# Operand address differences for TensorE, and the root of the first feed-forward, in a two-layer decoder trunk

## The chip, the cores and the metric

The kernel runs on 1 core of a Trainium2 chip. The metric is the device time of one execution in microseconds (us), lower is better.

## The reference, cut to what matters

```python
D_MODEL, SEQ, DEPTH, D_FF = 1024, 512, 2, 2816

def rms_norm(x, g):
    y = x * lax.rsqrt(jnp.mean(x * x, axis=-1, keepdims=True) + 1e-6)
    return y * g
def swiglu(x, wg, wu, wd):
    return (jax.nn.silu(x @ wg) * (x @ wu)) @ wd

for i in range(DEPTH):
    x = x + 0.5 * swiglu(rms_norm(x, ffn1_norm[i]), ffn1_w_gate[i], ffn1_w_up[i], ffn1_w_down[i])
    h = rms_norm(x, mix_norm[i])
    x = x + (conformer_conv(h, ...) if i % 2 == 0 else nsa_mixer(h, ...))
    x = x + 0.5 * swiglu(rms_norm(x, ffn2_norm[i]), ffn2_w_gate[i], ffn2_w_up[i], ffn2_w_down[i])
    gate = jax.nn.sigmoid(rms_norm(x, ple_norm[i]) @ ple_w_gate[i])
    x = x + gate * (p[i] @ ple_w_in[i])
return rms_norm(x, final_norm)
```

So there are four feed-forwards (two in each layer), one convolution module with a 31-tap depthwise filter, one block of sparse attention with three branches, two gates on a per-layer input, and a last norm. All of it is float32.

## The kernel before, in words

The activations are kept transposed: eight tiles of 128 features by 512 tokens (`self.xs`). Weights come from HBM in units of 128 x 1024 floats (4096 bytes in each partition) that `plan()` lays out in the order of use.

**Three matmuls for one.** TensorE multiplies in fp32r. Each float is therefore split into a high part (a copy into fp32r, on ScalarE) and a low part (the difference, on VectorE or GpSimd), and `mm3` (L360 to L365) issues three matmuls for each product: high by high (L363), weight high by activation low (L364), weight low by activation high (L365). The weight block (128 x 128) is the stationary operand and is loaded anew for each matmul; the activations (512 or 256 tokens) are the moving operand. The split weights stand in `wh` and `wl`, five buffers each (L299, L301, L323, L324).

**Full-size and half-size.** A plain product moves 512 tokens. In a feed-forward the first two column blocks of gate and up (`PLAIN = 2`) are plain. The other twenty go two by two through `pairs` (L502), seven products of half size in place of eight (Winograd's form of Strassen's scheme): its moving operands have 256 tokens. They are the high and low parts of the inputs (`s`, in slots), and sums of inputs `T1` to `T4` that `right_sums` (L482) makes (`px`). Its stationary operands are weight units ("s"), combinations of two units ("c" and "d", made in `combine` from the sums of `first_sums`), and a sum "e" that stands in a tile of its own, `s1hl`. The down products move 512 tokens of `hid`.

**Where operands stand.** An allocator stacks the pools one behind the other in each partition: constants, weights (2 + 5 + 5 buffers of 4096 bytes), a gap of 64 bytes (`gap0`), 24 slots of 2048 bytes, the small tiles of a norm (`tiny`, 832 bytes), a gap of 192 bytes (`gap1`), and then the pool of the phase, with gaps of 64 bytes ahead of `s1hl` and 192 ahead of `G` and `hid` (`PADS`). Taken modulo 256 bytes, the address of the moving operand less that of the stationary one is 64 for `s` and `px` against `wh` and `wl`, 192 for `px` against `s1hl`, and 0 for `hid` against `wh` and `wl`. Other tiles fall where they fall: the convolution's result (`tw`) against `wh` and `wl` has 32, the per-layer input (`zp`) 160, the attention's `e` tiles any multiple of 32, the probabilities against V 32.

**The order.** The program is written engine-neutral; a scheduler orders each engine's instructions by its own simulation, priorities (`high_priority`) and explicit constraints: `issue_after(x)` keeps what is inside behind instruction x in the order. All engines then work through fixed queues.

**The first feed-forward.** `ffn` (L550) of layer 0 starts on data straight from HBM. `rfin` (L468) has two steps: sums over features of the squares by eight small matmuls (`token_sums`, L452), plus epsilon on VectorE (L474), the power -0.5 on GpSimd (`rsqrt`, L445); then four transposes on TensorE that spread the root over the partitions (L458) and a copy (L465). The sums stand behind the third input of block 1's gate product (`SUMS_AT = 3`), the transposes behind the end of that product. The four `right_sums` come behind the last square and behind L474 (`vins`). `gated` (L565 to L568) multiplies and splits the plain blocks' results. `ahead` (L341) splits the weight units that come next, as far as the five buffers go.

Of the kernel before, what the change touches and what calls it, by code (L numbers as in the profile page):

```python
# [24 lines left out]
PAD_SLOTS, PAD_PHASE = 16, 48  # L25
PADS = {"s1hl": 16, "G": 48, "hid": 48}
# [11 lines left out]
SUMS_AT = 3  # L38
# [159 lines left out]
class Kern:  # L198
    def __init__(self, ctx, tc, aps):
        self.ctx, self.tc, self.nc = ctx, tc, tc.nc  # L200
        self.a = aps
        pool = lambda name, **kw: ctx.enter_context(tc.tile_pool(name=name, **kw))
        self.cpool = pool("consts", bufs=1)
        self.wpool = pool("weights", bufs=1)
        pool("gap0", bufs=1).tile([128, PAD_SLOTS], F32, name="gap0")
        self.spool = pool("slots", bufs=1)
        self.tiny = pool("tiny", bufs=2)
        pool("gap1", bufs=1).tile([128, PAD_PHASE], F32, name="gap1")
# [5 lines left out]
        self.HLB, self.held, self.now = 5, set(), None  # L214
        self.next_raw = self.next_split = 0
# [9 lines left out]

    def ptile(self, tag, n, w=512, dt=F32):
        if tag in PADS and tag not in self.padded:
            self.padded.add(tag)
            self.phase.tile([128, PADS[tag]], F32, name=f"gap{tag}{self.uid}", tag=f"gap{tag}", bufs=1)
        self.uid += 1  # L230
        return self.phase.tile([128, w], dt, name=f"{tag}{self.uid}", tag=tag, bufs=n)
# [38 lines left out]
    def halves(self):  # L270
        h = self.wpool.tile([128, HU], F32R, name=f"wh{self.uid}", tag="wh", bufs=self.HLB)
        l = self.wpool.tile([128, HU], F32R, name=f"wl{self.uid}", tag="wl", bufs=self.HLB)
        self.uid += 1
        return h, l

    def _split(self, what, j):
        nc = self.nc
        w = sum(x[2] for x in UNITS[j])
        if what == "r":
            t = self.wpool.tile([128, HU], F32, name=f"wr{j}", tag="wh", bufs=self.HLB)  # L280
# [10 lines left out]
        h, l = self.halves()  # L291
        name = UNITS[j][0][0][0]
        nsa, calm = name.startswith("nsa"), name.startswith(CALM)
        eng = nc.gpsimd if calm or nsa and j % 4 in L_POOL else nc.vector
        for c in self.pieces(j, w):
            if nsa and j % 4 in H_POOL:
                nc.gpsimd.tensor_copy(h[:, c], t[:, c])
            else:
                nc.scalar.activation(h[:, c], t[:, c], AF.Copy)  # L299
# [11 lines left out]
    def combine(self, what, j):  # L311


        nc = self.nc
        t, u = self.raw[j], self.raw[j + 1]
        lo, hi = slice(0, HU // 2), slice(HU // 2, HU)
        q = self.sums[j]
        if what == "c":
            nc.vector.tensor_tensor(q[:, lo], u[:, lo], t[:, lo], op=OP.subtract)
            nc.vector.tensor_tensor(u[:, lo], t[:, hi], q[:, lo], op=OP.subtract)  # L320
        src = q if what == "c" else u
        h, l = self.halves()
        nc.scalar.activation(h, src, AF.Copy)  # L323
        nc.vector.tensor_tensor(l, src, h.bitcast(F32), op=OP.subtract)  # L324
        self.hl[what, j] = (h, l)

    def first_sums(self, j):

        nc = self.nc
        t, u = self.raw[j], self.raw[j + 1]  # L330
        lo, hi = slice(0, HU // 2), slice(HU // 2, HU)
        q = self.sums[j] = self.ptile("sq", 2, HU)
        with self.tc.issue_after(self.summed):
            nc.vector.tensor_tensor(q[:, hi], t[:, lo], u[:, lo], op=OP.subtract)
        nc.vector.tensor_tensor(u[:, lo], u[:, lo], u[:, hi], op=OP.add)
        hl = self.ptile("s1hl", 2, HU, F32R)
        nc.scalar.activation(hl[:, lo], u[:, lo], AF.Copy)
        nc.vector.tensor_tensor(hl[:, hi], u[:, lo], hl[:, lo].bitcast(F32), op=OP.subtract)
        self.hl["e", j] = (hl[:, lo], hl[:, hi])

    def ahead(self, e):  # L341
# [3 lines left out]
        self.loads()  # L345
        while self.next_split < e:
# [100 lines left out]

    def token_sums(self, p, tiles):
# [19 lines left out]
    def rfin(self, acc):  # L468

        with self.tc.high_priority(FIN_PRI):  # L470
# [4 lines left out]
            r = self.rsqrt(v, 4)  # L475
# [74 lines left out]
    def ffn(self, n, i, nxt):  # L550
# [4 lines left out]
        fin = self.rfin(self.acc)  # L555
# [5 lines left out]
        for pi, fs in enumerate(PARTS):  # L561
# [9 lines left out]
            if pi == 0:  # L571
                assert PLAIN == 2
                first = (n, i) == (1, 0)
                wait = []
                for f in range(PLAIN):
                    pg, pu = self.bank(), self.bank()
                    if f == 0:
                        for ks in (range(KD - 1), (KD - 1,)):
                            plain(pg, g, f, ks)
                            plain(pu, u, f, ks)  # L580
                    for p, nm in ((pg, g), (pu, u)) if f else ():
                        if first and p is pg:
                            plain(p, nm, f, range(SUMS_AT))
                            with self.tc.issue_after(self.lastmm):
                                next(fin)
                            plain(p, nm, f, range(SUMS_AT, KD))
                        else:
                            plain(p, nm, f)
# [16 lines left out]
                for f, pg, pu in wait:  # L605
                    gr = self.tmp()
                    nc.vector.tensor_tensor(pg, pg, R, op=OP.mult)
                    nc.scalar.activation(gr, pg, AF.Silu)
                    gated(f, gr, pu)
            for f in fs[::2]:  # L610
# [3 lines left out]
                G = next(both)  # L614
# [104 lines left out]
    def glu(self, c, pa, pg, ta=None):  # L719
# [4 lines left out]
        with self.tc.high_priority(FIN_PRI):  # L724
            nc.vector.tensor_tensor(pg, pg, self.R, op=OP.mult)
            nc.scalar.activation(pg, pg, AF.Sigmoid, bias=self.col("conv_b_pw1", KD + c))
            if CONV_ON[c] == "pe":
                u = self.ptile("uu", 2, PH * (SP + LAGS - 1)).rearrange("p (q s) -> p q s", q=PH)
# [4 lines left out]
            else:  # L733
                u = self.ptile("u", 3, S + TAPS - 1)
# [103 lines left out]
    def conv(self, nxt):  # L838
# [3 lines left out]
        self.dwc = self.phase.tile([128, KD, TAPS], F32, name="dwc")  # L842
# [159 lines left out]
    def put_k(self, g):  # L1002
        nc, t, KT = self.nc, self.kt, self.KTs[g % 2]
        for br, sl, ot in ((0, slice(0, 64), slice(64, 128)), (1, slice(64, 128), slice(0, 64))):
            nc.scalar.activation(KT[sl, 0, br, 32:], t[sl], AF.Copy)
            nc.vector.tensor_tensor(KT[sl, 1, br, 32:], t[sl], KT[sl, 0, br, 32:].bitcast(F32), op=OP.subtract)
            nc.sync.dma_start(KT[ot, :, br, 32:].bitcast(F32), KT[sl, :, br, 32:].bitcast(F32))
# [6 lines left out]
    def proj_q(self, g, pr):  # L1014
# [6 lines left out]
        Q = self.phase.tile([128, 2, 512], F32R, name=f"q{g}{pr}", tag="q", bufs=4)  # L1021
# [60 lines left out]
    def cmp_in(self, j, first):  # L1082
# [15 lines left out]
        for gp, p in wait:  # L1098
            for s in range(2):
                t = self.ptile("e", EB, 516)  # L1100
# [54 lines left out]
    def scores(self, job):  # L1155
# [16 lines left out]
        for a in range(HPG):  # L1172
            Q = self.Q[g, a // 2][:, a % 2, qt * 128:qt * 128 + 128]
            src, e = {}, self.slot() if a == HPG - 1 else self.ptile("e", EB, 516)
# [109 lines left out]
    def osplit(self, g):  # L1284
        nc = self.nc
        for pr in range(2):
            t = self.OT[g][pr]
            h, l = (self.slot(F32R) if g < 2 else self.ptile("e", EB, 516, F32R)[:, :512] for _ in range(2))
# [26 lines left out]
    def nsa(self, nxt):  # L1315
# [3 lines left out]
        P = self.phase  # L1319
# [3 lines left out]
        self.pos = P.tile([128, 2, 16], F32, name="pos")  # L1323
        nc.gpsimd.dma_start(self.pos, self.a["pos"])
        self.rowmask = P.tile([128, 1], F32, name="rowmask")
        nc.gpsimd.dma_start(self.rowmask, self.a["rowmask"])
        self.gates = P.tile([128, 4, 48], F32, name="gates")
        self.gates0 = P.tile([128, 16], F32, name="gates0")
        self.kc = P.tile([128, G, 32], F32, name="kc")
        self.ec = P.tile([128, 4, HPG, 32], F32, name="ec")  # L1330
        nc.gpsimd.memset(self.ec, 0.0)
        self.vc = P.tile([128, G, 128], F32R, name="vc")
        self.KTs = [P.tile([128, 2, 2, 544], F32R, name=f"kt{i}") for i in range(2)]
        self.Vs = [P.tile([128, 8, 128], F32R, name=f"v{i}") for i in range(2)]
        self.ects = [P.tile([128, 2, 512], F32R, name=f"ect{i}") for i in range(2)]
# [111 lines left out]
    def run(self):  # L1447
        def phase():
            self.padded = set()
# [4 lines left out]
        for i in range(L):  # L1454
            self.tb = 4
# [84 lines left out]
```

## Time and profile before

| | us |
|---|---|
| median of 3 runs | 1990.7 (1990.41 to 1990.72) |
| the profiled execution | 1990.31 |
| its span, first to last instruction | 1988.2 |
| granted clock of TensorE, mean | 0.997 of full speed |

In the profile PE is TensorE's matmuls, PEld its weight loads, DVE VectorE, ACT ScalarE, POOL GpSimd, SP the engine that issues DMAs. A row of a group says: line, engine, operation, output tile <- input tiles, shape, count, then busy us and mean ns of one, and the idle time before them with what ended it. A row of the timeline says: start in us, length in us, and the same names. The recorded length of a matmul includes its way through the array; how fast matmuls follow each other is read from their starts.

### The profile page before, as it was taken

What the parts mean: (1) busy time and instruction counts of PE and PEld (TensorE: products, weight loads), DVE (VectorE), ACT (ScalarE), POOL (GpSimd) and SP (SyncE); (2) the same over time, 40 slices, a digit from 0 to 9 for tenths busy, and PEclk for the clock granted to TensorE, in tenths of its full rate; (3) what the DMA queues carried; (4) which work ended last, traced back from release to release, by engine and by line L of the source; (5) the groups of instructions that cost most, each with busy time, mean ns of one, the idle gap of its engine ahead of it and who ended that gap; (6) DMA issues with size and microseconds to landing.
All of it is one profiled execution on the core that took longest, in us unless ns stands there. A gap on an engine that the chain in (4) does not pass through costs nothing.

```text
span 1988.2 us, 32709 instructions
## 1 busy us (share of the span) xinstructions
PE 1961.4 (99%) x12534; PEld 1760.0 (89%) x12534; DVE 1544.6 (78%) x2703; ACT 1099.8 (55%) x1972; POOL 331.0 (17%) x365
## 2 busy tenths in 40 slices
PE   8999999999999999999999999999999999999998
PEld 7989898888789898988999989888888789998987
DVE  8869777795688796877978868636889797786875
ACT  7636446663565363545644626337888665363543
POOL 0000000352300000022000000557666200000022
PEclk9999999999999999999999999999999999999999
DMA  4332322566425243343232323463332023232241
GB/s 172 107 106 97 128 86 96 192 206 202 138 99 172 88 151 128 99 138 117 85 126 87 129 84 100 156 196 106 89 96 101 23 94 129 96 117 96 96 149 53
DMA packets 79483, 235.16 MB, mean 118 GB/s; under 512 B 8848, under 2 KB 16160, under 8 KB 79328
## 3 DMA queue, kind: packets, MB, share of 16 engines
q1 hardware_dynamic: 78368, 230.69, 35.4%
q8 instruction: 98, 1.61, 0.3%
q0 software_dynamic: 816, 2.33, 0.3%
q14 instruction: 57, 0.47, 0.1%
q10 hardware_dynamic: 144, 0.07, 0.0%
HBM read 214.66 MB, written 16.29 MB: 116 GB/s over the span
## 4 chain that ended last, share of the span: by engine, by line
PE 90%; DVE 6%; ACT 1%; issue 1%; DMA 1%; SPq 0%; POOL 0%; DVEq 0%; ACTq 0%; POOLq 0%
PE b L363 27%; PE b L364 27%; PE b L365 27%; PE b L828 2%; PE b L1187 1%; PE b L1251 1%; DMA raw<-in_w 1%; PE b L1270 1%; PE b L1271 1%; PE b L1126 1%; DVE s L422 1%; DVE t L489 1%; DVE wl L301 1%; DVE px L498 0%; DVE acc L439 0%
## 5 line engine op out<-in xcount | busy, mean ns | idle before, releaser
L363 PE MATMUL b<-s,wh 128*128 128x256 f32 (+1 forms) x1408 | 443.8, 316 | 2.2 <-ACT wh L299 1.4
L364 PE MATMUL b<-s,wh 128*128 128x256 f32 (+1 forms) x1408 | 440.9, 314 | 1.4 <-DVE s L422 1.2
L365 PE MATMUL b<-s,wl 128*128 128x256 f32 (+1 forms) x1408 | 440.2, 314 | 0.1
L299 ACT ACTIVATE wh<-raw 128x1024 fp32r<-128x1024 f32 (+1 forms) x251 | 263.7, 1053 | 241.8 <-PE b L364 158.4
L364 PE MATMUL b<-px,wh 128*128 128x256 f32 (+1 forms) x1112 | 319.8, 288 | 1.7 <-DVE px L498 1.7
L363 PE MATMUL b<-px,wh 128*128 128x256 f32 (+1 forms) x1112 | 319.4, 288 | 0.7 <-ACT G L510 0.7
L365 PE MATMUL b<-px,wl 128*128 128x256 f32 (+1 forms) x1112 | 319.6, 288 | 0.0
L301 DVE TENSOR_TENSOR wl<-raw,wh 128x1024 fp32r<-128x1024 f32 (+1 forms) x205 | 251.6, 1229 | 65.2 <-ACT wh L299 64.8
L363 PEld LDWEIGHTS b<-s,wh 128*128 128x128 f32 x1408 | 264.5, 188 | 21.2 <-ACT wh L299 2.2
L364 PEld LDWEIGHTS b<-s,wh 128*128 128x128 f32 x1408 | 264.3, 188 | 20.4 <-DVE s L422 2.3
L365 PEld LDWEIGHTS b<-s,wl 128*128 128x128 f32 x1408 | 263.4, 188 | 18.6 <-DVE wl L301 0.5
L364 PE MATMUL b<-hid,wh 128*128 128x512 f32 x704 | 273.1, 389 | 0.0
L365 PE MATMUL b<-hid,wl 128*128 128x512 f32 x704 | 272.7, 389 | 0.0
L363 PE MATMUL b<-hid,wh 128*128 128x512 f32 x704 | 269.1, 389 | 0.0
L301 POOL TENSOR_TENSOR wl<-raw,wh 128x1024 fp32r<-128x1024 f32 (+1 forms) x53 | 128.5, 2429 | 695.2 <-ACT wh L299 695.1
L510 ACT ACTIVATE G<-b 128x256 f32<-128x256 f32 x400 | 144.5, 376 | 132.4 <-PE b L365 109.8
L364 PEld LDWEIGHTS b<-px,wh 128*128 128x128 f32 x1112 | 208.7, 188 | 7.1 <-DVE px L498 2.3
L363 PEld LDWEIGHTS b<-px,wh 128*128 128x128 f32 x1112 | 208.4, 188 | 6.1 <-ACT G L510 1.3
L365 PEld LDWEIGHTS b<-px,wl 128*128 128x128 f32 x1112 | 208.8, 188 | 4.0
L364 PEld LDWEIGHTS b<-hid,wh 128*128 128x128 f32 x704 | 132.1, 188 | 27.0
L365 PEld LDWEIGHTS b<-hid,wl 128*128 128x128 f32 x704 | 132.0, 188 | 27.1
L363 PEld LDWEIGHTS b<-hid,wh 128*128 128x128 f32 x704 | 132.1, 188 | 26.9
(246 smaller groups left out, 3621.0 us busy)
## 6 DMA issues: line engine op xcount, KB each, us to landing
raw<-in_w SPq DMA_DIRECT2D x255, 512.0 KB, 3.3
rawx<-in_w SPq DMA_DIRECT2D x80, 512.0 KB, 3.3
tw<-in_tw SPq DMA_DIRECT2D x20, 576.0 KB, 6.6
skew<-table SPq DMA_DIRECT2D x16, 320.0 KB, 5.8
z<-t SPq DMA_DIRECT2D x16, 256.0 KB, 2.4
hid<-z SPq DMA_DIRECT2D x16, 256.0 KB, 3.9
tt<-skew SPq DMA_DIRECT2D x16, 256.0 KB, 2.9
wr<-in_w SPq DMA_DIRECT2D x8, 512.0 KB, 4.0
```

The lines of the kernel that those rows point to most:

```text
L299: nc.scalar.activation(h[:, c], t[:, c], AF.Copy)
L301: eng.tensor_tensor(l[:, c], t[:, c], h[:, c].bitcast(F32), op=OP.subtract)
L363: mm(out, sh, mh, start=start, stop=False, **how)
L364: mm(out, sh, ml, start=False, stop=False, **how)
L365: self.lastmm = mm(out, sl, mh, start=False, stop=stop, **how).ins
L422: b = nc.vector.scalar_tensor_tensor(view(l), x, g, view(h.bitcast(F32)), op0=OP.mult, op1=OP.subtract)
L489: sub = lambda o, x, y: nc.vector.tensor_tensor(o, x, y, op=OP.subtract)
L510: copy = lambda o, x: nc.scalar.activation(o, x, AF.Copy)
L828: nc.tensor.matmul(p[:, q * SP:q * SP + SP], T[q][:, d * 128:d * 128 + 128], u[:, q, o:o + SP], start=d == 0, stop=d == LAGS - 1)
L1126: nc.tensor.matmul(P[mh][:, :124], w, B[kk // 4][:, kk % 4, :], start=kk == 0, stop=kk == 15)
L1187: nc.tensor.matmul(p[:, :32 - lo + nk], Q, KT[:, i, "sw".index(b), lo:32 + nk], start=i == 0, stop=i == 1)
L1251: nc.tensor.transpose(p[:, a * 128:a * 128 + 128], J[a, b][:, kt * 128:kt * 128 + 128], self.ident)
```

## The change

It has two parts.

*Addresses.* Every tile's place is now chosen. `tiny` moves ahead of the weights, a gap of 64 bytes follows it, and slots stand right behind the weights. The split units get 256 bytes more, and a unit made for `pairs` (a "s" unit of a pair, "c" and "d") begins 64 bytes (`TURN` = 16 floats) further on. `place` puts the first tile of a tag at a chosen address modulo 256 (`AT`), and several widths become multiples of 256 bytes (`UW` = 576 floats; KT and the e tiles). With this the moving operand less the stationary one is 192 modulo 256 for all of `pairs`, and 0 for the products of 512 tokens, the convolution's, the per-layer input's and the attention's among them.

*First feed-forward of layer 0.* The root is Newton's iteration on VectorE (ten instructions on 128 x 4) in place of GpSimd's power. The sums of squares move ahead of the eighth input of block 0's two products. The first `right_sums` waits for the sum of squares alone, the other three for the root. Splitting of the first pair's units is held back (`cap`), the sums of its weights (`first_sums`, `sum_parts`) come later (`lazy`), and the gates of the plain blocks come behind the right sums. In layer 0's first phase there are five `t` buffers, not four.

```diff
-PAD_SLOTS, PAD_PHASE = 16, 48
-PADS = {"s1hl": 16, "G": 48, "hid": 48}
+PAD, TURN = 16, 16
+AT = {"s1hl": 192, "px": 128, "hid": 128, "tw": 128, "e": 128, "tt": 0, "q": 0}
+UW = 576
-SUMS_AT = 3
+NEWTON = 3
...
+    def place(self, tag, size, at=None):
+        pad = 0 if at is None else (at - self.top) % 256
+        if pad:
+            self.uid += 1
+            self.phase.tile([128, pad // 4], F32, name=f"gap{tag}{self.uid}", tag=f"gap{tag}", bufs=1)
+        self.top += pad + -(-size // 32) * 32
...
-    def halves(self):
-        h = self.wpool.tile([128, HU], F32R, name=f"wh{self.uid}", tag="wh", bufs=self.HLB)
+    def halves(self, half=False):
+        o = TURN if half else 0
+        h = self.wpool.tile([128, HU + 64], F32R, name=f"wh{self.uid}", tag="wh", bufs=self.HLB)[:, o:o + HU]
...
         if pair:
-            with self.behind():
-                self.first_sums(j)
+            if j not in self.lazy:
+                with self.behind():
+                    self.first_sums(j)
+                    self.sum_parts(j)
...
+        if lazy:
+            with self.tc.issue_after(self.righted):
+                self.sum_parts(j)
+                nc.vector.tensor_tensor(u[:, lo], t[:, hi], q[:, lo], op=OP.subtract)
...
+    def root_steps(self, v, n):
+        y = self.tiny.tile([128, 4], F32, name="r", tag="r")[:, :n]
+        a = self.tiny.tile([128, 4], F32, name="ra", tag="ra")[:, :n]
+        nc.vector.tensor_scalar(y.bitcast(I32), v.bitcast(I32), -0.5, float(0x5f3759df), op0=OP.mult, op1=OP.add)
+        for _ in range(NEWTON):
+            nc.vector.tensor_tensor(a, y, y, op=OP.mult)
+            nc.vector.scalar_tensor_tensor(a, a, -0.5, v, op0=OP.mult, op1=OP.mult)
+            self.root = nc.vector.scalar_tensor_tensor(y, a, 1.5, y, op0=OP.add, op1=OP.mult).ins
...
                         for ks in (range(KD - 1), (KD - 1,)):
                             plain(pg, g, f, ks)
                             plain(pu, u, f, ks)
+                            if first and len(ks) > 1:
+                                with self.tc.issue_after(self.lastmm):
+                                    next(fin)
...
-                        if first and p is pg:
-                            plain(p, nm, f, range(SUMS_AT))
-                            with self.tc.issue_after(self.lastmm):
-                                next(fin)
-                            plain(p, nm, f, range(SUMS_AT, KD))
...
                 if first:
-                    with self.tc.issue_after(self.squared), self.tc.issue_after(self.vins):
-                        for k in range(KD // 2):
+                    for k in range(KD // 2):
+                        with self.tc.issue_after(self.squared), self.tc.issue_after(self.root if k else self.summed):
                             self.right_sums(f"ffn{n}_norm", i, k)
+                        if k == KD // 2 - 2:
+                            self.cap = ENTRY["s", self.lazy[1]] + 1
+                            with self.tc.issue_after(self.root):
+                                self.ahead(ENTRY["s", self.lazy[1]])
+                    self.cap = None
...
+                with self.tc.issue_after(self.root) if first and f == PLAIN else nullcontext():
+                    G = next(both)
+                if first and f == PLAIN:
+                    with self.tc.issue_after(self.righted):
+                        plain_gates()
...
-            self.tb = 4
+            self.tb = 5 if i == 0 else 4
```

More of the change, by code (lines that the diff above doesn't have):

```diff
@@ L213, in __init__ @@
         self.unskewed = []
-        self.HLB, self.held, self.now = 5, set(), None
+        self.HLB, self.held, self.now, self.cap = 5, set(), None, None
+        self.lazy = ()
         self.next_raw = self.next_split = 0
@@ L224, in tmp, with own @@
         return self.ptile("t", self.tb, dt=dt)
+    def place(self, tag, size, at=None):
[4 more added lines that the diff above has]
+        self.top += pad + -(-size // 32) * 32
+    def own(self, name, shape, dt=F32, at=None):
+        size = 4
+        for n in shape[1:]:
+            size *= n
+        self.place(name, size, at)
+        return self.phase.tile(shape, dt, name=name)
     def ptile(self, tag, n, w=512, dt=F32):
-        if tag in PADS and tag not in self.padded:
-            self.padded.add(tag)
-            self.phase.tile([128, PADS[tag]], F32, name=f"gap{tag}{self.uid}", tag=f"gap{tag}", bufs=1)
+        if tag not in self.tags:
+            self.tags.add(tag)
+            self.place(tag, n * (-(-w * 4 // 32) * 32), AT.get(tag))
         self.uid += 1
@@ L290, in _split @@
             del self.raw[j]
-        h, l = self.halves()
+        h, l = self.halves(pair)
         name = UNITS[j][0][0][0]
@@ L316, in combine @@
         lo, hi = slice(0, HU // 2), slice(HU // 2, HU)
+        lazy = what == "c" and j in self.lazy
+        if lazy:
+            self.first_sums(j)
         q = self.sums[j]
@@ L319, in combine @@
             nc.vector.tensor_tensor(q[:, lo], u[:, lo], t[:, lo], op=OP.subtract)
[L320 removed]
+            if not lazy:
+                nc.vector.tensor_tensor(u[:, lo], t[:, hi], q[:, lo], op=OP.subtract)
         src = q if what == "c" else u
[L322 removed]
+        h, l = self.halves(True)
         nc.scalar.activation(h, src, AF.Copy)
@@ L335, in first_sums, with sum_parts @@
         nc.vector.tensor_tensor(u[:, lo], u[:, lo], u[:, hi], op=OP.add)
+    def sum_parts(self, j):
+        nc = self.nc
+        u = self.raw[j + 1]
+        lo, hi = slice(0, HU // 2), slice(HU // 2, HU)
         hl = self.ptile("s1hl", 2, HU, F32R)
@@ L345, in ahead @@
         self.loads()
+        if self.cap is not None:
+            e = min(e, self.cap)
         while self.next_split < e:
@@ L466, in spread, with rfin @@
         return R
-    def rfin(self, acc):
+    def rfin(self, acc, steps=False):
         with self.tc.high_priority(FIN_PRI):
@@ L474, in rfin @@
             self.vins = self.nc.vector.tensor_scalar(v, p, 1e-6, None, op0=OP.add).ins
-            r = self.rsqrt(v, 4)
+            r = (self.root_steps if steps else self.rsqrt)(v, 4)
         yield
@@ L554, in ffn @@
         self.now, self.T4 = (f"ffn{n}", i), []
-        fin = self.rfin(self.acc)
+        first = (n, i) == (1, 0)
+        if first:
+            self.lazy = [PLACE[nm, i, 0, PLAIN][0] for nm in (g, u)]
+            self.cap = ENTRY["s", self.lazy[0]]
+        fin = self.rfin(self.acc, steps=first)
         def plain(p, nm, f, ks=range(KD)):
@@ L604, in ffn, with plain_gates @@
                 R = self.R
[L605 to L609, printed above, removed]
+                def plain_gates():
+                    for f, pg, pu in wait:
+                        gr = self.tmp()
+                        nc.vector.tensor_tensor(pg, pg, R, op=OP.mult)
+                        nc.scalar.activation(gr, pg, AF.Silu)
+                        gated(f, gr, pu)
+                if not first:
+                    plain_gates()
             for f in fs[::2]:
@@ L613, in ffn @@
                 both = self.pairs((g, u), i, f)
-                G = next(both)
+                with self.tc.issue_after(self.root) if first and f == PLAIN else nullcontext():
+                    G = next(both)
+                if first and f == PLAIN:
+                    with self.tc.issue_after(self.righted):
+                        plain_gates()
                 nc.vector.tensor_tensor(G, G, R[:, None, :].to_broadcast([128, 2, 512]), op=OP.mult)
@@ L841, in conv @@
         X, U, Y = self.X, {}, []
-        self.dwc = self.phase.tile([128, KD, TAPS], F32, name="dwc")
+        self.dwc = self.own("dwc", [128, KD, TAPS])
         nc.gpsimd.dma_start(self.dwc, self.a["dwc"])
@@ L1287, in osplit @@
             t = self.OT[g][pr]
-            h, l = (self.slot(F32R) if g < 2 else self.ptile("e", EB, 516, F32R)[:, :512] for _ in range(2))
+            h, l = (self.slot(F32R) if g < 2 else self.ptile("e", EB, UW, F32R)[:, :512] for _ in range(2))
             nc.scalar.activation(h, t, AF.Copy)
@@ L1322, in nsa @@
             nc.gpsimd.dma_start(self.xd[m * 128:m * 128 + 128, :], self.xs[m])
-        self.pos = P.tile([128, 2, 16], F32, name="pos")
+        self.pos = self.own("pos", [128, 2, 16])
         nc.gpsimd.dma_start(self.pos, self.a["pos"])
-        self.rowmask = P.tile([128, 1], F32, name="rowmask")
+        self.rowmask = self.own("rowmask", [128, 1])
         nc.gpsimd.dma_start(self.rowmask, self.a["rowmask"])
[L1327 to L1330, printed above, removed]
+        self.gates = self.own("gates", [128, 4, 48])
+        self.gates0 = self.own("gates0", [128, 16])
+        self.kc = self.own("kc", [128, G, 32])
+        self.ec = self.own("ec", [128, 4, HPG, 32])
         nc.gpsimd.memset(self.ec, 0.0)
[L1332 to L1335, printed above, removed]
+        self.vc = self.own("vc", [128, G, 128], F32R, at=0)
+        self.KTs = [self.own(f"kt{i}", [128, 2, 2, UW], F32R, at=128) for i in range(2)]
+        self.Vs = [self.own(f"v{i}", [128, 8, 128], F32R, at=0) for i in range(2)]
+        self.ects = [self.own(f"ect{i}", [128, 2, 512], F32R, at=0) for i in range(2)]
         for t in self.KTs:
```

36 lines of the change are left out of this document (18 added, 18 removed).

## The prediction

> **What bounds the kernel now.** I read the page first, then the groups of TensorE's instructions by form, the timeline of single matmuls, and last the waits and the timeline of the first 90 us. The page:
>
> ```profile
> span 1988.2 us, 32709 instructions
> PE 1961.4 (99%) x12534; PEld 1760.0 (89%) x12534; DVE 1544.6 (78%) x2703; ACT 1099.8 (55%) x1972; POOL 331.0 (17%) x365
> PE 90%; DVE 6%; ACT 1%; issue 1%; DMA 1%; SPq 0%; POOL 0%; DVEq 0%; ACTq 0%; POOLq 0%
> ```
>
> TensorE has a record at nearly all times, and 90% of the chain that ended last is its own. So the time is the number of matmuls by the distance from one start to the next, plus a few pauses. The change leaves the number alone. The groups by form give the numbers of each kind:
>
> ```profile
> L364 PE MATMUL b<-px,wh 128*128 128x256 f32 x1008 | 278.9, 277 | 1.7 <-DVE px L498 1.7
> L364 PE MATMUL b<-hid,wh 128*128 128x512 f32 x704 | 273.1, 389 | 0.0
> L363 PE MATMUL b<-s,wh 128*128 128x256 f32 x960 | 265.7, 278 | 1.0 <-ACT wh L299 1.0
> L364 PE MATMUL b<-s,wh 128*128 128x512 f32 x448 | 175.9, 393 | 1.4 <-DVE s L422 1.2 <-DVE s L1290 0.2
> L364 PE MATMUL b<-px,s1hl 128*128 128x256 f32 x320 | 88.1, 277 | 0.2 <-DVE px L498 0.2
> L364 PE MATMUL b<-px,wh 128*128 128x512 f32 x104 | 40.9, 393 | 0.0
> L364 PE MATMUL b<-tw,wh 128*128 128x512 f32 x64 | 25.1, 395 | 0.0
> L364 PE MATMUL b<-zp,wh 128*128 128x512 f32 x32 | 12.7, 396 | 0.0
> L365 PE MATMUL b<-e,wl 128*128 128x512 f32 x32 | 12.6, 394 | 0.0
> ```
>
> L363, L364 and L365 have the same counts, so each stands for three. Half-size (256 tokens): 3 x (1008 + 960 + 320) = 6864. Full-size at difference 0 (`hid`): 2112. At 64 (`s`, `px`): 3 x (448 + 104) = 1656. At 32 (`tw`): 192. At other differences (`zp`, `e`): 192.
>
> **The full-size matmuls.** Three undisturbed runs, first and last start of each; there are 133, 167 and 150 steps between the two:
>
> ```profile
> 225.02 0.39 PE L365 MATMUL b<-hid,wl 128*128 128x512 f32 x1
> ...
> 255.16 0.39 PE L363 MATMUL b<-hid,wh 128*128 128x512 f32 x1
> ```
> ```profile
> 908.00 0.39 PE L364 MATMUL b<-px,wh 128*128 128x512 f32 x1
> ...
> 946.23 0.39 PE L365 MATMUL b<-s,wl 128*128 128x512 f32 x1
> ```
> ```profile
> 515.03 0.39 PE L363 MATMUL b<-tw,wh 128*128 128x512 f32 x1
> ...
> 550.03 0.39 PE L363 MATMUL b<-tw,wh 128*128 128x512 f32 x1
> ```
>
> At difference 0: 30.14 us / 133 = 226.6 ns. At 64: 38.23 / 167 = 228.9. At 32: 35.00 / 150 = 233.3. The change takes all to 0. That is worth 1656 x 2.3 = 3.8 us, 192 x 6.7 = 1.3 us, and for `zp` and `e` between 192 x 2.3 and 192 x 6.7, say 0.9: together 6.0 us. A third of the 1656 and the `e` stand in attention, where TensorE also waits for other engines; I take half of their share away and count **5 us**, bounds 3.8 and 6.
>
> The Trainium skill, page "SBUF — State Buffer", section "Who interferes with whom", gives TensorE two independent read ports, one for the moving operand and one for weights, and says that only the port pair of VectorE and GpSimd causes contention. By that rule both address terms are nil. The trace disagrees: 226.6 against 228.9 and 233.3 ns for one shape of matmul.
>
> **The half-size matmuls** have two distances from start to start, and keep either for long. Three stretches of 59, 6 and 23 steps:
>
> ```profile
> 142.08 0.28 PE L364 MATMUL b<-s,wh 128*128 128x256 f32 x1
> ...
> 149.03 0.28 PE L363 MATMUL b<-px,wh 128*128 128x256 f32 x1
> ```
> ```profile
> 149.74 0.28 PE L363 MATMUL b<-px,s1hl 128*128 128x256 f32 x1
> ...
> 150.42 0.28 PE L363 MATMUL b<-px,s1hl 128*128 128x256 f32 x1
> ```
> ```profile
> 1642.69 0.28 PE L363 MATMUL b<-px,s1hl 128*128 128x256 f32 x1
> ...
> 1645.39 0.28 PE L365 MATMUL b<-px,s1hl 128*128 128x256 f32 x1
> ```
>
> The first, at difference 64, is wide: 6.95 us / 59 = 117.8 ns. The second is the `s1hl` product behind it, difference 192: 0.68 us / 6 = 113.3. The later products of that stage stay at 113.3, back at difference 64. By starts, 1643 of the 6864 are wide; the first and the last of them are these:
>
> ```profile
> 35.75 0.28 PE L363 MATMUL b<-s,wh 128*128 128x256 f32 x1
> ...
> 1975.69 0.28 PE L365 MATMUL b<-px,wl 128*128 128x256 f32 x1
> ```
>
> Each stage of pairs begins wide when it comes from full-size products, and the quick pace comes nearly always where `s1hl` begins; no undisturbed stretch falls back. But the third fence is a product at 192 that stays wide: 2.70 us / 23 = 117.4. So 192 does not by itself end a stretch of 117.8 ns; what the trace doesn't show is a stage that *enters* at 192. Bounds: all quick, 1643 x 4.45 ns = 7.3 us won; all wide, (6864 - 1643) x 4.45 = 23.2 us lost. I take the quick end, since 192 is where the pace changed for the better and never for the worse, less 0.5 for matmuls that stand in pauses anyway: **6.8 us** won.
>
> **The first feed-forward.** Its pauses:
>
> ```profile
> PE b L458 <- POOL r L445: 3.8, 2, 2.6
> PE b L364 <- DVE px L498: 1.9, 3, 0.8
> ```
> ```profile
> 23.13:51.50 28.37, 23.70 (x152) 20.56 (x150) 28.30 (x45) 19.31 (x30) 1.41 (x1) 1.00 0.28 94
> 51.50:90.00 38.50, 38.50 (x338) 38.41 (x339) 38.18 (x58) 26.08 (x43) 0.00 (x0) 1.00 0.34 112
> ```
>
> The columns of the second fence are length, then PE, PEld, DVE, ACT and POOL. From 23.13 to 51.5 TensorE has no record for 28.37 - 23.70 = 4.67 us, and VectorE rests for 0.07. VectorE is the limit there, and it still has 38.18 of 38.50 behind. So a gain must come out of its queue:
>
> ```profile
> 19.33 0.62 PE L363 MATMUL b<-s,wh 128*128 128x512 f32 x2
> 19.64 2.28 DVE L439 TENSOR_TENSOR acc<-acc,t 128x512 f32<-128x512 f32 x3
> 23.13 0.69 DVE L334 TENSOR_TENSOR sq<-raw,rawx 128x512 f32<-128x512 f32 x1 [1.21 <-DMA raw<-in_w]
> ```
> ```profile
> 26.19 0.95 PE L452 MATMUL b<-meanr,acc 128*128 128x1 f32 x8
> 28.06 0.16 DVE L474 TENSOR_SCALAR v<-b 128x4 f32<-128x4 f32 x1
> 28.31 1.41 POOL L445 TENSOR_TENSOR r<-v,power 128x4 f32<-128x4 f32 x1 [26.31 <-DVE v L474]
> 29.77 0.65 PE L458 MATMUL b<-ident,r 128*128 128x128 f32 x4 [2.63 <-POOL r L445]
> 35.62 1.29 DVE L607 TENSOR_TENSOR b<-b,R 128x512 f32<-128x512 f32 x2
> 45.24 0.70 DVE L565 TENSOR_TENSOR b<-b,t 128x512 f32<-128x512 f32 x1
> ```
>
> - *Newton.* Ten VectorE instructions by 0.16 us (L474's row, the same size) are 1.6 us, against 1.41 on GpSimd and hops of under 0.1 each way. The root itself takes as long as before; but 1.6 us more stand in the full queue, ahead of everything that waits there.
> - *Sums earlier.* The squares' total is there at 19.64 + 2.28 = 21.92; the sums run at 26.19 and TensorE then waits 2.63 for the root. Before the eighth input is enough to take that wait away. Bound on the other side: the 42 matmuls of block 0's first seven inputs are issued by 19.33, and if the sums stand in TensorE's queue right there, it waits 21.92 - 19.3 = 2.6 for the total, and nothing is won.
> - *Right sums earlier, gates and weight sums later.* The 1.21 us that VectorE waits for a unit's DMA at 23.13 can go to the first right sums. The plain gates (1.29 for both, then L565 and L568, of one size, at 0.70 for each of two blocks: 4.1 us) move behind the right sums, where only the down products wait for them. Splits that are held back hold their raw buffers and so SP's loads behind them longer; hidden as long as VectorE is the later of the two.
>
> For VectorE's queue ahead of the last right sum: -1.2 - 4.1 + 1.6 = -3.7 us. If all that is put off comes due before 90 us, where it has 0.3 us of room, the sum is +1.6 - 1.2 = +0.4. I take **2.5 us** won, nearer the first end, since the down products that wait for the gates come behind three pairs.
>
> **The sum**, against the profiled execution's own 1990.31 us (2.1 over its span, 0.4 under the median): -5 - 6.8 - 2.5 = -14.3, so **1976 us**. Its own range is 1971 to 1981: the bounds of the full-size term, pauses of the first feed-forward between +0.4 and -5, and a part of the stages entering wide.
>
> **Rivals.**
> 1. *Half-size products locked at 117.8 ns* (slower than before). Now the change of difference at `s1hl` is what ends a stretch of 117.8 ns. With 192 everywhere, no such change is left in a stage. If entry at 192 is wide, as it is at 64, it stays: 1990.3 - 5 - 2.5 + 23.2 = 2006. It decides from the point at which more than (7.3 + 7.5) / 30.5 = 48% of the half-size matmuls are wide. For it speaks the third fence above; against it the second.
> 2. *As many wide as before.* Phases at the entries fall by luck, and about a quarter stays wide: 1990.3 - 7.5 = 1983.
> 3. *Addresses don't matter,* and the distances belong to stages, not to differences; that is the rule named above. Then only the first feed-forward is left: 1988. Against it: `px` at full size has 228.9 where `hid` has 226.6, with the same weights' buffers.
> 4. *The first feed-forward loses.* TensorE waits 2.6 us for the total in place of the root, and 1.6 us of Newton lengthen VectorE's queue, so that the px wait grows by it: +1.6 in place of -2.5, 1980.
>
> **How the numbers follow.** Chances: forecast 0.62, rival 1 0.16, rival 2 0.12, rival 3 0.04, rival 4 0.06. A measurement of this kernel tells about 0.2% (4 us) from no change. The first, third and fifth cases lie under 1986.7, rival 3 at the edge, rival 1 above 1994.7, with a tail of half-wide outcomes between: faster 0.80, same 0.05, slower 0.15. The range is 1969 to 1987: it takes in the forecast's and the cases 2 and 4, 0.80 together, and leaves out rival 1.
>
> **What would show it.** `s`, `px`, `tw` and `zp` full-size matmuls at 226.7 ns from start to start, as `hid`. Half-size ones at 113.3 ns from a stage's first product on (mean length 276 ns in the groups in place of 277 and 278). L458 no longer waits in the first 40 us, and the wait for L498 is shorter. I am wrong if a stage of pairs runs at 117.8 ns from end to end, or if TensorE's time without a record between 20 and 90 us is over 4.7 us.

## The result, and the profile after

| | median us | lowest to highest | runs |
|---|---|---|---|
| before | 1990.7 | 1990.41 to 1991.97 | 5 |
| after | 2008.2 | 2007.63 to 2010.23 | 5 |

The ratio is 1.0089, 95% interval 1.0074 to 1.0103: slower, where 1976 was forecast. The page of the changed kernel (profiled execution 2007.63 us):

```profile
span 2005.8 us, 32695 instructions
PE 1977.3 (99%) x12534; PEld 1780.5 (89%) x12534; DVE 1547.0 (77%) x2713; ACT 1099.9 (55%) x1972; POOL 336.1 (17%) x364
PE 88%; DVE 7%; ACT 2%; issue 1%; DMA 1%; POOL 0%; SPq 0%; DVEq 0%; ACTq 0%; POOLq 0%
```

TensorE has as many matmuls as before and is busy for 15.9 us more. The groups by form say which (L397 to L399 are `mm3` now):

```profile
L398 PE MATMUL b<-px,wh 128*128 128x256 f32 x1008 | 282.5, 281 | 0.9 <-DVE px L544 0.8
L398 PE MATMUL b<-hid,wh 128*128 128x512 f32 x704 | 273.2, 389 | 0.0
L397 PE MATMUL b<-s,wh 128*128 128x256 f32 x960 | 268.5, 281 | 0.8 <-ACT wh L315 0.4 <-ACT G L556 0.3
L398 PE MATMUL b<-px,s1hl 128*128 128x256 f32 x320 | 89.3, 280 | 0.0
L398 PE MATMUL b<-px,wh 128*128 128x512 f32 x104 | 40.7, 391 | 0.0
```

The half-size ones grew from 277 and 278 ns to 280 and 281, `s1hl`'s from 277 to 280; `hid` stands where it stood, and `px` at full size went down from 393 to 391. The timeline shows a stage of pairs, from its first matmul to its last:

```profile
139.97 0.39 PE L399 MATMUL b<-hid,wl 128*128 128x512 f32 x1
140.20 0.28 PE L397 MATMUL b<-s,wh 128*128 128x256 f32 x1
...
219.23 0.28 PE L399 MATMUL b<-px,wl 128*128 128x256 f32 x1
219.35 0.40 PE L397 MATMUL b<-hid,wh 128*128 128x512 f32 x1
```

672 steps in 219.35 - 140.20 = 79.15 us: 117.8 ns from end to end, the sign by which the prediction said that it would be wrong. And the full-size products of `px` and `s`:

```profile
912.96 0.39 PE L397 MATMUL b<-px,wh 128*128 128x512 f32 x1
...
952.88 0.39 PE L399 MATMUL b<-s,wl 128*128 128x512 f32 x1
```

176 steps, 226.8 ns each, where the same products had 228.9. `tw` has 226.8 as well.

Below, a half-size matmul is called wide when the distance to the next start is between 115.5 and 125 ns. By that count 1643 of the 6864 products of pairs were wide before, and 5883 are now. The counts further down take in the attention's 32 matmuls of 256 tokens as well; with them it is 1666 before and 5908 now, of 6896. Summed over all undisturbed distances, half-size matmuls cost 19.1 us more than before and full-size ones about 4.7 us less (4.4 to 4.9, by where undisturbed ends). One more change was in no case of the prediction. In layer 1's first feed-forward, before and after:

```profile
947.91 0.16 DVE L474 TENSOR_SCALAR v<-b 128x4 f32<-128x4 f32 x1
948.15 1.39 POOL L445 TENSOR_TENSOR r<-v,power 128x4 f32<-128x4 f32 x1 [35.53 <-DVE v L474]
```
```profile
954.23 0.15 DVE L520 TENSOR_SCALAR v<-b 128x4 f32<-128x4 f32 x1
954.46 8.81 POOL L479 TENSOR_TENSOR r<-v,power 128x4 f32<-128x4 f32 x1 [35.27 <-DVE v L520]
961.71 0.69 DVE L370 TENSOR_TENSOR s1hl<-rawx,s1hl 128x512 fp32r<-128x512 f32 x1
963.32 0.65 PE L504 MATMUL b<-ident,r 128*128 128x128 f32 x4 [3.66 <-POOL r L479]
964.64 1.30 DVE L660 TENSOR_TENSOR b<-b,R 128x512 f32<-128x512 f32 x2 [2.24 <-ACT R L511]
```

GpSimd's power takes 8.81 us in place of 1.39, and TensorE waits 3.66 us for it. It ends at 963.27, 0.87 us behind L370's end at 962.40, and up to there VectorE had no gap since v. What TensorE's distances ahead of 80 us have over the usual ones sums up to 9.6 us, where it was 11.3; that is the first feed-forward. So the account of the span's 17.6 us is 19.1 (half-size) - 4.7 (full-size) + 3.7 (the wait for the power) - 1.7 (first feed-forward) = 16.4; the other 1.2 were not traced.

### The profile page after: what moved, and what is told of

It reads as the page before. It is cut to its first block, busy times and chain, and to the rows that moved or that the text cites. A ratio compares the mean times of both kernels' runs of the same rounds, so it can differ in the third digit from the quotient of the medians.

```text
span 2005.8 us, 32695 instructions
## 1 busy us (share of the span) xinstructions
PE 1977.3 (99%) x12534; PEld 1780.5 (89%) x12534; DVE 1547.0 (77%) x2713; ACT 1099.9 (55%) x1972; POOL 336.1 (17%) x364
## 4 chain that ended last, share of the span: by engine, by line
PE 88%; DVE 7%; ACT 2%; issue 1%; DMA 1%; POOL 0%; SPq 0%; DVEq 0%; ACTq 0%; POOLq 0%
PE b L397 27%; PE b L398 27%; PE b L399 27%; PE b L888 2%; PE b L1247 1%; PE b L1311 1%; PE b L1186 1%; PE b L1330 1%; PE b L1331 1%; DMA raw<-in_w 1%; DVE t L535 1%; DVE wl L317 1%; DVE wl L346 1%; DVE s L456 1%; DVE px L544 0%
## 5 line engine op out<-in xcount | busy, mean ns | idle before, releaser
L397 PE MATMUL b<-s,wh 128*128 128x256 f32 (+1 forms) x1408 | 446.1, 318 | 1.6 <-ACT wh L315 1.1
L399 PE MATMUL b<-s,wl 128*128 128x256 f32 (+1 forms) x1408 | 443.2, 316 | 0.2 <-DVE wl L317 0.2
L397 PE MATMUL b<-px,wh 128*128 128x256 f32 (+1 forms) x1112 | 323.0, 291 | 1.4 <-ACT G L556 1.4
L398 PE MATMUL b<-px,wh 128*128 128x256 f32 (+1 forms) x1112 | 323.3, 291 | 0.9 <-DVE px L544 0.8
L399 PE MATMUL b<-px,wl 128*128 128x256 f32 (+1 forms) x1112 | 322.9, 291 | 0.8 <-DVE wl L346 0.8
L397 PEld LDWEIGHTS b<-s,wh 128*128 128x128 f32 x1408 | 264.9, 188 | 20.3 <-ACT wh L315 2.0
L399 PEld LDWEIGHTS b<-s,wl 128*128 128x128 f32 x1408 | 264.3, 188 | 17.7 <-DVE wl L317 0.5
L399 PE MATMUL b<-hid,wl 128*128 128x512 f32 x704 | 272.8, 389 | 0.0
L397 PE MATMUL b<-hid,wh 128*128 128x512 f32 x704 | 269.3, 389 | 0.0
L397 PEld LDWEIGHTS b<-px,wh 128*128 128x128 f32 x1112 | 209.3, 188 | 6.5 <-ACT G L556 2.0
L399 PEld LDWEIGHTS b<-px,wl 128*128 128x128 f32 x1112 | 209.8, 189 | 4.9 <-DVE wl L346 1.0
L399 PEld LDWEIGHTS b<-hid,wl 128*128 128x128 f32 x704 | 132.1, 188 | 27.2
L397 PEld LDWEIGHTS b<-hid,wh 128*128 128x128 f32 x704 | 132.2, 188 | 26.9
```

Of the source, the lines that this page charges most:

```text
L397: mm(out, sh, mh, start=start, stop=False, **how)
L398: mm(out, sh, ml, start=False, stop=False, **how)
L399: self.lastmm = mm(out, sl, mh, start=False, stop=stop, **how).ins
```

## The experiments

**Which address term, and what about it?** Three kernels move only operands of half-size products; each engine's order is that of the changed kernel. A `TURN` of 48 floats in place of 16 gives the difference 64 in place of 192. Theory A is rival 1's: a stage comes in wide, and only a change of difference inside it ends that. In its narrow form only the step from 64 up to 192 does. Theory B: 192 itself is the slow difference. Theory C: the half-size pace doesn't depend on these addresses.

```diff
-PAD, TURN = 16, 16
+PAD, TURN = 16, 48
```


> The changed kernel with TURN 48 in place of 16: half-size products of pairs have difference 64, s1hl keeps 192; full-size ones stay at 0, and the order of every engine is that of the changed kernel. Theory A (a stage that comes from full-size products enters wide, 117.8 ns, and only a change of difference inside it can end that; 192 everywhere took that change away): wide ones fall from 5883 to about 1643 as before, 4240 x 4.45 ns = 19 us off: 1989. Theory B (192 itself is the slow difference, with or without a change): the main products at 64 run quick from their start and only the 960 of s1hl are wide: (5883 - 960) x 4.45 = 22 us off, 1986. Theory C (the half-size pace doesn't depend on these addresses; the 512-token operands at other places set it): 2008.

```diff
-PAD, TURN = 16, 16
-AT = {"s1hl": 192, ...
+PAD, TURN = 16, 48
+AT = {"s1hl": 64, ...
```


> The changed kernel with TURN 48 and s1hl at 64 too: all half-size products of pairs at difference 64, none at 192, full-size ones at 0. Theory A (no change of difference in a stage, so nothing ends the wide entry): as the changed kernel, 2008, nearly every stage at 117.8 ns from end to end. Theory B (192 is the slow one): quick throughout, (5883 x 4.45 = 26 us off) 1982. Theory C: 2008.

```diff
-AT = {"s1hl": 192, ...
+AT = {"s1hl": 64, ...
```


> The changed kernel with s1hl alone moved from 192 to 64: half-size products at 192 and the s1hl product at 64, the mirror of what the kernel before has. Theory A in its general form (any change of difference shakes the pace): about 1989. Theory A in its narrow form (only the step from 64 up to 192 shortens the distance, the step back down lengthens it): 2008 or a little more. Theory B (192 is slow, 64 quick): the 960 products of s1hl go quick, 960 x 4.45 = 4 us off, 2004.

The fourth has the new addresses and the old first feed-forward:

```diff
-        fin = self.rfin(self.acc, steps=first)
+        fin = self.rfin(self.acc)
...
+                        if first and p is pg:
+                            plain(p, nm, f, range(SUMS_AT))
```


> The changed kernel's addresses with the first feed-forward as before (GpSimd's power, sums behind the third input of block 1's gate, gates ahead of the pairs, four t buffers); every engine's order is that of the kernel before. If the first feed-forward's part is worth the 1.7 us that the pauses ahead of 80 us show, and the long power (8.81 us, 3.7 us of TensorE's wait) at 954 us of the changed kernel is a chance of that one execution: 2008.2 + 1.7 = 2010. If the long power comes from GpSimd having its first power only at 366 us, it isn't there with the power back at 28 us: 2006. If the first feed-forward's part costs more than it wins: under 2005.

Measured, ratios against the kernel before on the same chip: 64 with `s1hl` at 192, 1990.0 us (1.0005, 0.9995 to 1.0014). All at 64, 2011.7 (1.0113, 1.0096 to 1.0130). 192 with `s1hl` at 64, 1988.3 (0.9996, 0.9987 to 1.0006). Addresses alone, 2010.7 (1.0110, 1.0095 to 1.0125).

64 with `s1hl` at 192 is quick again, so C is out. All at 64 is no quicker than all at 192, so B is out. The addresses alone are the slow part. The mirror (192 with `s1hl` at 64) isn't slow, which speaks for A's general form by time. Its timeline says otherwise (192 until 268.65, `s1hl` at 64 until 271.48, then 192 again):

```profile
260.29 0.28 PE L397 MATMUL b<-s,wh 128*128 128x256 f32 x1
...
268.77 0.28 PE L397 MATMUL b<-px,s1hl 128*128 128x256 f32 x1
...
271.48 0.28 PE L399 MATMUL b<-px,s1hl 128*128 128x256 f32 x1
271.60 0.28 PE L397 MATMUL b<-px,wh 128*128 128x256 f32 x1
...
286.44 0.28 PE L399 MATMUL b<-px,wl 128*128 128x256 f32 x1
```

72 steps to 268.77 are 117.8 ns; the 23 between the two `s1hl` rows are 117.8 too; the 131 from 271.60 on are 113.3. The step down to 64 changed nothing, and the step back up to 192, at the end of `s1hl`, did. I count the steps with wide products ahead of them (seven at the least) and no pause near. Over this run the step down left the pace wide in 15 of 15 cases, and the step up made it quick in 13 of 13. So the narrow form has the directions right, and my number for it (2008) was wrong, because every `s1hl` has a step up behind it. The step up isn't certain, though: in the kernel before, where it stands at the entry of `s1hl`, the same count gives 11 of 17. The third fence of the prediction on half-size matmuls is one of the six that stayed wide, and no run shows what sets them apart. The idea that the power's 8.81 us come from GpSimd having its first power late fell as well: with that power back at 28 us (1.41 us there), the one in layer 1 still took 8.81.

**The distances by themselves.** A kernel of 14,869 matmuls and nothing of the trunk:

```diff
+    for seg in segments():
+        n, a, b, c, count = seg
+        ow, ol, ox = -a % 256 // 4, -c % 256 // 4, (b - a) % 256 // 4
+        for i in range(0, count, 3):
+            k = i // 3 % 8 * 128
+            h, l = W[0][:, ow + k:ow + k + 128], W[1][:, ol + k:ol + k + 128]
+            for st, mv in ((h, X[0][:, :n]), (h, X[1][:, ox:ox + n]), (l, X[0][:, :n])):
+                nc.tensor.matmul(p[:, :n], st, mv, start=True, stop=True)
```


> Nothing of the trunk is computed: 14,869 fp32r matmuls on TensorE alone, each with a weight block of its own, in runs of one size and one address difference (all multiples of 32 modulo 256), each run behind 24 to 30 matmuls of 512 tokens at difference 0; then changes from every difference to every other inside half-size runs, alternating differences, entries behind 24 to 29 full-size ones, and entries behind a pause. Theory A narrow (the pace at the entry of a half-size run is wide at 64 and at 192; a step from 64 to 192 shortens it to 113.3 ns, the step from 192 to 64 leaves it): runs at 64 and 192 behind full-size ones at 117.8, 0 at 119.9; 64 then 192 gives 113.3, 192 then 64 stays at 117.8, each in the same way every time it is tried. Rival (the state is set by other engines' accesses or by the phase at which a run begins, not by the step): entries behind 24, 25, ... 29 full-size matmuls differ, or 64 then 192 stays wide. Full-size at 0, 64 and 32: 226.7, 228.9 and 233.3.

`ow` and `ol` shift the stationary operands (the weights), `ox` the moving operand of each product's second matmul. Six stretches of its timeline; a row's length less 0.28 us, divided by its count less one, is the distance:

```profile
676.26 5.23 PE L84 MATMUL p<-x,w 128*128 128x256 f32 x43
682.83 6.74 PE L84 MATMUL p<-x,w 128*128 128x256 f32 x58
```
```profile
1167.03 5.23 PE L84 MATMUL p<-x,w 128*128 128x256 f32 x43
1172.81 7.93 PE L84 MATMUL p<-x,w 128*128 128x256 f32 x66
```
```profile
2012.97 5.46 PE L84 MATMUL p<-x,w 128*128 128x256 f32 x45
2020.77 4.47 PE L84 MATMUL p<-x,w 128*128 128x256 f32 x38
```

Difference 64 behind full-size products: 4.95 / 42 = 117.9 ns; 192 behind that: 6.46 / 57 = 113.3. In the second fence 192 comes first: 117.9, then 64: 117.7. The third is difference 64 ahead of and behind a pause (1.47 us from the last start to the next): 117.7, then 113.2. The same numbers by table, ns between starts once the stretch is steady, state before in the rows, difference now in the columns; each step between half-size stretches stands there once, and the weights move in it:

| behind | 0 | 64 | 128 | 192 |
|---|---|---|---|---|
| full size at 0 | 120.0 | 117.8 | 120.0 | 117.8 |
| half size at 0 | - | 113.3 | 118.7 | 117.8 |
| 64, wide | 120.0 | - | 118.6 | 113.3 |
| 128 | 120.0 | 117.8 | - | 113.3 |
| 192, wide | 120.0 | 117.8 | 118.7 | - |

Of these four only 64 and 192 reach 113.3, and what came before decides whether they do. Entries at 0, 64, 128 and 192 behind 24, 27 and 30 full-size matmuls, 24 in all, have the distance of the table's first row each time, with the other engines idle. So the rival is out: other engines aren't needed, and the moment of the entry made no difference, as far as entries three matmuls apart can tell. Full-size: 226.7 at 0, 228.9 at 64, 233.3 at 32, and no multiple of 32 is better than 0.

The same kernel sets a limit to the narrow form. Three stretches change the difference inside each product of three matmuls: 64, 64, 192 by the weights; then 64, 192, 64 and 192, 64, 192 by the moving operand:

```profile
1487.80 9.46 PE L84 MATMUL p<-x,w 128*128 128x256 f32 x82
1603.22 11.23 PE L84 MATMUL p<-x,w 128*128 128x256 f32 x94
1620.11 11.12 PE L84 MATMUL p<-x,w 128*128 128x256 f32 x93
```

The first runs at 113.3 ns, the other two at 117.7 and 117.8 from end to end, though each of their products has a step from 64 up to 192 too. So the difference alone doesn't tell: every step up that made the pace quick here was one of the weights' address.

**Using it.** If the step up is the cause, bringing it forward must shorten the wide part of each stage to the products ahead of it: 96 of them for the mirror above, 72 for 64 with `s1hl` at 192, 48 if the combined units stand at 192, and hardly any if high and low weights alternate. `halves` takes the offsets of the high and of the low part in floats (one number for both); 48 gives difference 64, 16 gives 192.

```diff
-        h, l = self.halves(pair)
+        h, l = self.halves(48 if pair else 0)
...
-        h, l = self.halves(True)
+        h, l = self.halves(16)
```


> The changed kernel with the pairs' single units at difference 64 and the combined units and s1hl at 192: each stage comes in at 64 and steps up to 192 behind its first 48 half-size products; the order of every engine is that of the changed kernel. Theory A narrow (the step from 64 up to 192 is what ends 117.8 ns): some 17 x 48 = 816 to 1200 wide ones in place of 2012 with 64 and s1hl at 192 (1990.0): 1986. Theory A general (any change, in either direction, with some chance): about the same, but a part falls back to 117.8 at each of the many steps down, 1988 to 1995. Rival (only s1hl's tile itself does it, by standing in another pool): as the changed kernel, 2008.

```diff
-        h, l = self.halves(pair)
+        h, l = self.halves(*((48, 16) if pair else ()))
...
-        h, l = self.halves(True)
+        h, l = self.halves(48, 16)
```


> The changed kernel with the high parts of the pairs' weights at difference 64 and the low parts at 192, so that each product of three matmuls has 64, 64, 192 and the step up comes in every product; the order of every engine is that of the changed kernel. Theory A narrow, with a step down that does no harm: quick from the second product of each stage on, under 200 wide ones, 2008.2 - 5700 x 4.45 ns = 25 us off: 1983. If the step down costs what the step up wins: an own pace between 113.3 and 119.9 from end to end, 1983 to 2015.

| half-size differences | wide in the stage at 260 us | wide in all | us | 2008.2 - (5908 - wide) x 4.45 ns |
|---|---|---|---|---|
| all 64 | all | 6816 | 2011.7 | 2012.2 |
| all 192 (the changed kernel) | all | 5908 | 2008.2 | - |
| 64, `s1hl` 192 | 74 | 2012 | 1990.0 | 1990.9 |
| 192, `s1hl` 64 | 96 | 1742 | 1988.3 | 1989.7 |
| single units 64, the rest 192 | 50 | 1270 | 1987.5 | 1987.6 |
| high parts 64, low parts 192 | 2 | 387 | 1983.8 | 1983.6 |

The count of wide ones gives every time within 1.4 us. The kernel before took 1990.7 us in the changed kernel's series, 1989.1 in that of the rows with 2011.7, 1990.0 and 1988.3, and 1990.2 in that of the last two; by the ratios the agreement is within 1.1 us. The alternating kernel in the stage that the changed kernel ran at 117.8 ns, 671 steps of 113.3:

```profile
139.86 0.28 PE L397 MATMUL b<-s,wh 128*128 128x256 f32 x1
...
215.91 0.28 PE L399 MATMUL b<-px,wl 128*128 128x256 f32 x1
```

Ratios of the last two: 0.9985 (0.9976 to 0.9994) and 0.9971 (0.9958 to 0.9984).

**The long power.** First, Newton's root there too, on the layout of the mirror:

```diff
-        fin = self.rfin(self.acc, steps=first)
+        fin = self.rfin(self.acc, steps=first or (n, i) == (1, 1))
```


> Half-size at 192 and s1hl at 64 as in the run at 1988.3, and in layer 1's first feed-forward the root is Newton's on VectorE too, in place of the one GpSimd power of 8.81 us that ended only 0.87 us after VectorE's queue first stood still. Theory P (that power is kept waiting by VectorE's unbroken queue, a cost of the new addresses or of a fine timing that comes with them, 3.7 us on TensorE and more behind): the pause goes, 4 to 5.5 us off: 1983 to 1984.5. Rival (the wait for the root hides another that is due at the same time): 1987 to 1988.

1994.9 us (1.0023, 1.0013 to 1.0033); against the mirror's 0.9996 that is 5.4 us more. Both expectations missed:

```profile
943.88 0.15 DVE L520 TENSOR_SCALAR v<-b 128x4 f32<-128x4 f32 x1
948.43 0.16 DVE L487 TENSOR_SCALAR r<-v 128x4 int32<-128x4 int32 x1
952.98 0.15 DVE L489 TENSOR_TENSOR ra<-r 128x4 f32<-128x4 f32 x1
...
959.72 0.16 DVE L491 SCALAR_TENSOR_TENSOR r<-ra,r 128x4 f32<-128x4 f32 x1
959.94 1.12 PE L504 MATMUL b<-ident,r 128*128 128x128 f32 x4 [10.62 <-DVE r L491]
```

From v to the last of ten instructions of 0.16 us 16 us pass, since the order puts others of 0.68 and 1.21 us between them, and TensorE waits 10.6 us. The mechanism of the power was not tested by this. The next kernels, on the alternating weights, do that; the first lets VectorE wait for GpSimd, the second moves v and r:

```diff
+            if (self.now, steps) == (("ffn1", 1), False):
+                s = self.tiny.tile([128, 4], F32, name="ra", tag="ra")
+                self.nc.vector.tensor_copy(s, r)
+                r = s
```


> The alternating weights (1983.8), and in layer 1's first feed-forward VectorE copies the four columns of the root from GpSimd, so that its queue stands still some nine instructions behind v until GpSimd's power is through. Theory P (the power is held up until VectorE's queue stands still, and ends 0.87 us after): it ends about 0.9 us behind the instruction ahead of that copy, in 5.3 to 5.6 us in place of 8.8; TensorE's wait falls from 4.0 us to under 1; 1980.5. Rival (the power's length belongs to GpSimd, its memory or code, and VectorE's pause is a consequence): it keeps 8.8 us, VectorE waits at the copy some 3.5 us, and the time is 1984 to 1987.

```diff
+        pool("gap0", bufs=1).tile([128, PAD], F32, name="gap0")
         self.tiny = pool("tiny", bufs=2)
-        pool("gap0", bufs=1).tile([128, PAD], F32, name="gap0")
```


> The alternating weights with the gap of 64 bytes moved from behind the norm's small tiles to ahead of them: v and r stand where they stand modulo 256 in the kernel before (32 and 96), and nothing else moves. If the address of the small tiles makes GpSimd's power long: 1.4 us again, TensorE's 4.0 us of wait gone, 1979.5. If it is the timing against VectorE's queue: 8.8 us as before and 1983.8.

With the copy (1982.3 us; 0.9963, 0.9950 to 0.9977), the timeline of GpSimd and VectorE:

```profile
941.72 5.27 POOL L479 TENSOR_TENSOR r<-v,power 128x4 f32<-128x4 f32 x1 [35.27 <-DVE v L520]
...
945.44 0.68 DVE L539 TENSOR_TENSOR t<-G 128x512 f32<-128x512 f32 x1
947.02 0.17 DVE L524 COPY ra<-r 128x4 f32<-128x4 f32 x1 [0.91 <-POOL r L479]
947.25 0.65 PE L504 MATMUL b<-ident,ra 128*128 128x128 f32 x4 [0.32 <-DVE ra L524]
```

L539 ends at 946.12, the power at 946.99: again 0.87 us later, and 5.27 us long in place of 8.8. TensorE's wait is 0.3. So in these kernels the power lasts until VectorE's queue pauses. The time fell by less than the wait: by 1.7 us against the 1984.0 of the kernel below, in the same series, where 3.3 us of wait are gone; where the rest went was not traced. With v and r at their old places modulo 256 it stays 8.81 us, and the time 1984.0 (0.9974, 0.9963 to 0.9984): the small tiles' place isn't what does it.

**The first feed-forward alone,** on the alternating weights:

```diff
-        fin = self.rfin(self.acc, steps=first)
+        fin = self.rfin(self.acc)
```


> The alternating weights with the first feed-forward as in the kernel before; every engine's order but GpSimd's last ones is that of the kernel before. It gives the first feed-forward's part by itself, on a half-size pace that is quick from the start: if the part is worth what the pauses ahead of 80 us show (11.3 before, 9.6 after), this is 1983.8 + 1.7 = 1985.5; by the forecast's term 1986.3; if it is worth nothing, 1983.8.

1986.1 us (0.9983, 0.9974 to 0.9992) with the old one, against 1984.0 with the new one in the same series (the kernel with v and r moved): it is worth 2.2 us. Single runs of the two lie at 1984.9 to 1989.3 and 1983.5 to 1986.1.

## Why the prediction was wrong, point by point

- *Full-size matmuls, 5 us won:* right, about 4.7 by the distances.
- *Half-size matmuls, 6.8 us won:* this step failed, in its sentence "I take the quick end, since 192 is where the pace changed for the better and never for the worse". 19.1 us were lost, with 5883 of 6864 products wide. It was not the place, 192, but the way there: each `s1hl` brought the step from 64 to 192, and with 192 everywhere there is no step left. The third fence (192 and 117.4 ns) was evidence that a stretch at 192 can be wide, and "each stage of pairs begins wide when it comes from full-size products" already said what entry does; the second fence showed a step and was read as a state. Rival 1 had the mechanism, and its chance of 0.16 gave the third fence too little weight. That its 2006 is only 2 us from the result is luck: it has 23.2 us for the half-size matmuls where 19.1 came, and nothing for the power below, 3.7.
- *First feed-forward, 2.5 us won:* right in sum, 2.2. The views of it, sums, first and last step of the root, and transposes:

```profile
22.10 1.05 PE L498 MATMUL b<-meanr,acc 128*128 128x1 f32 x8 [1.19 <-DVE acc L473]
23.48 0.15 DVE L520 TENSOR_SCALAR v<-b 128x4 f32<-128x4 f32 x1
23.67 0.17 DVE L487 TENSOR_SCALAR r<-v 128x4 int32<-128x4 int32 x1
27.43 0.16 DVE L491 SCALAR_TENSOR_TENSOR r<-ra,r 128x4 f32<-128x4 f32 x1
28.58 0.60 PE L504 MATMUL b<-ident,r 128*128 128x128 f32 x4
```

  The wait of 2.63 us for the root is gone, and one of 1.19 for the total has come, less than half of the 2.6 that was the bound. Newton's steps take 27.59 - 23.67 = 3.9 us, not 1.6: I had summed their lengths, as if nothing stood between them. It cost nothing here, since TensorE had block 1 to work on. The -5 that the range has for this term isn't worked out; the prediction's own terms give -3.7.
- *Not foreseen:* the long power, 3.7 us of TensorE's wait. It comes with the addresses (it is there with the old first feed-forward too).
- *The sum:* even with the half-size step put right the forecast isn't reached. The alternating kernel is 5.8 us faster than the kernel before (0.9971), not 14.3. The power's 3.6 us of wait are part of what lacks; with its 387 wide ones the half-size term is (1666 - 387) x 4.45 ns = 5.7 us, not 6.8. The rest wasn't traced.
- *Rivals 2, 3 and 4* are out: 86% of the half-size products were wide, the addresses do decide, and the first feed-forward won.

What stays open is why the same power got in between VectorE's instructions after 1.39 us in the kernel before, with the same row of instructions there. It was 8.8 us in every kernel with the new addresses that left VectorE's queue alone. Which address, or whether a difference in timing does it, no run told apart, except that v's and r's place modulo 256 is not it.

## What to carry to other kernels

A pace that changes at a place in the code may belong to the change and not to the value it changes to: before a layout makes a value constant everywhere, look for one stretch that *enters* at that value, and if there is none, measure the transitions in a kernel of matmuls alone. And a small operation on GpSimd or a chain of small ones on VectorE costs what the queue around it makes of it, not the sum of its own lengths.

## What the runs showed of the hardware

- The distance of half-size matmuls (256 tokens, fp32r, a weight block for each) at one and the same difference, 64 or 192, is 113.3 or 117.8 ns, by what came before. In the kernel of matmuls alone a step of the weights from 64 to 192 makes it quick, the step back from a wide stretch leaves it wide, and a pause of 1.5 us makes it quick too; alternating 64, 64, 192 by the weights it is quick from the second product on. Alternating by the moving operand it stays at 117.7 and 117.8, and in the trunk before the change the step up did it in 11 of 17 cases. At 0 it is 120.0 whatever came before. The Trainium skill, page "SBUF — State Buffer", section "Who interferes with whom", lets only the port pair of VectorE and GpSimd contend. In the kernel of matmuls alone TensorE's distance changes with the addresses of its own operands all the same, 113.3 to 120.0 ns, with VectorE and GpSimd idle.
- A GpSimd instruction that lasts 1.0 to 1.4 us elsewhere lasted 8.8 us while VectorE ran tensor_tensor instructions without a gap. It ended 0.87 us after the first gap, in the changed kernel and in the one with the gap put earlier. The same section says that a tensor_tensor with two inputs in SBUF contends with GpSimd's reads, and that the later one is blocked until the earlier has finished. The trace agrees on who blocks whom, but the block lasted for a row of twelve instructions, not for one; and in the kernel before the same row didn't hold it up (1.39 us).
